# Gate products made early on four row groups and kept in DRAM, GLA and attention regrouped into fewer TensorE visits, x split in halves

## The chip, the cores and the metric

One core of one Trainium2 chip runs the whole program. The metric is the device time of one execution in microseconds (us). TensorE (PE) does the matrix products, VectorE (DVE) and ScalarE (ACT) read its results out of PSUM and do the arithmetic, GpSimd (POOL) helps with sums, and SyncE (SP) issues nearly all DMA transfers, in one queue, in order.

## The reference, cut to what matters

One layer of a decoder over 2048 prompt tokens and 64 sample tokens (8 sequences of 8), 2112 in all, in f32:

```python
z = einsum('btd,dn->btn', x, w_in)              # 1024 -> 6928: q k v g_att gq gk gv g_gla g_lr r_att r_gla
o_att = swa(q, k, v, cache, sink, rel_table)    # 8 heads of 64, 2 KV heads, window 128, blocks of 128
log_a = log_sigmoid(g_lr @ w_gk_up + b_gk) / 16 # the gate product: rank 16 -> 512 = 4 heads x 128
# GLA, 4 heads, state S (128 x 256) carried from chunk to chunk, b = cumsum(log_a) in the chunk:
qt, kt, kend = q * exp(b), k * exp(-b), k * exp(b_last - b)
o = qt @ S + tril(qt @ kt.T) @ v
S = exp(b_last) * S + kend.T @ v
o_gla = rms_norm(o) * gla_norm_w
h = sigmoid(r_att) * ((o_att * silu(g_att)) @ w_pa) + sigmoid(r_gla) * ((o_gla * silu(g_gla)) @ w_pg)
y = layer_norm(alpha * x + h @ w_o)
```

The state of the 8 sample sequences is updated too, and keys, values and states are returned.

## The kernel before, in words

**Dense stream.** The big projections are eight passes, in this order: AT (attention's q, k, v and gate), G0, G1, G2 (GLA's k, q, v and gate for the four heads), PA (w_pa), RA, RG (the merge gates), PG (w_pg); a last stage multiplies by w_o. Each pass uses a seven-product Strassen-like scheme, so it has 21 units (7 products `i` x 3 token ranges `s` of 2 x 352 tokens), and a unit has 5 (AT) or 4 output blocks `p`. One block is one **group**: 12 matmuls of 128x128 weights on 352 columns (L1164 to L1166; 6 in PA), because every f32 operand is split into a rounded high part and a rest (`split`, L146: a cast on ACT, then a subtraction on DVE), and hi*hi, hi*lo, lo*hi are summed. The units' token side is read from DRAM (`raw_x`, L197), and split into `xh` and `xl` of 128x1408 (`prep_x`, L221) one unit ahead; some split pairs are kept in DRAM (`sp_d`) and only reloaded. Results go to DVE and ACT (`combine`, L251), which read them from four PSUM banks named `pd`.

**Side work.** After every group (every second one in PA) `tick()` advances a counter and traces what was put on that count with `at(t, fn)`. So a **visit** of TensorE to side work stands between two groups, and "n ticks later" means n groups later. All side work shares four other PSUM banks, `pa`. TensorE's order is exactly the traced one (`manual_schedule`); the order on the other engines and in SP's queue is chosen by the framework's scheduler when the program is built.

- *Setup and low-rank gate input*, in pass AT: `xcombo` (L553) makes g_lr and stores it to `gl_d` (DRAM, 32 rows: 16, twice).
- *Attention*, in G0 (`ta` = two ticks before G0): 16 blocks, one each SB = 7 ticks. At the block's tick o: `att_scores(.., 0)`, at o+1 `att_scores(.., 2)` (L614: 4 products each on 64-row halves of the array, two banks each; softmax follows behind the second on DVE and ACT), at o+6 and o+7 `att_trans` for each KV head (L651: 8 transposes, two banks each), at o+9 `att_out` (L666, one bank).
- *GLA*, from G1's second half to PG: four heads one after another (`chain`, L1031), 16 tiles of 128 tokens each, one tile each `st` = 4.36 ticks, in 9 chunks per head (`GCH`: 7 of 256 tokens, one of 128, one of 128 + 64). Per chunk: `gla_load` (L858: g_lr rows and k, q), `gla_z` (L878: the gate product for 32 rows x up to 256 columns on TensorE, then log-sigmoid, cumulative sum and exponentials on ACT and DVE), `gla_kq`. Per tile: **v** = `gla_v` (L921: three transposes, one bank, copied out by ACT at L929), **a** = `gla_a` (L934: one product, one bank, masked out by DVE at L939), **b** = `gla_b` (L952: three products of 256 columns, two banks: the output `op`, normalized by ACT and POOL, and the new state `sp`, taken up by DVE at L967), **c** = `gla_c` (L971: two transposes, one bank, multiplied out by DVE at L977).

f32 products of the side work run as two passes on TensorE, and transposes as one.

```python
    def tick():                                          # L132
        while side.get(now[0]):
            side[now[0]].pop(0)()
        now[0] += 1
    ...
            b = t0 + st * (c0 // P)                      # L1039, in chain
            at(b - 14, lambda B=B: gla_load(B))
            at(b - 10, lambda B=B: gla_z(B))
    ...
                at(o, lambda B=B, i=i: gla_v(B, i))
                at(o + st / 4, lambda B=B, i=i: gla_a(B, i))
                at(o + 3 * st / 4, lambda B=B, i=i: gla_b(B, i))
                at(o + 15 * st / 8, lambda B=B, i=i: gla_c(B, i, P, i * P))
```

Of the kernel before, what the change touches and what calls it, by code (L numbers as in the profile page):

```python
# [16 lines left out]
ALU = mybir.AluOpType  # L17
# [40 lines left out]
def kernel(ctx, tc, io):  # L58
# [96 lines left out]
    class Pass:  # L155
# [314 lines left out]
    as_per = const.tile([NS, NS], F32, name="asper")  # L470
    wg = const.tile([P, KT, 32], F32, name="wg")
    for t, n in ((wg, "w_glr"), (cmask, "c_causal"), (smask, "c_scausal"), (bsel, "c_bsel"),
# [332 lines left out]
    for c in range(NP // AT):  # L805
# [41 lines left out]
    def unit(dt=F32, name="u"):  # L847
        return mt("u", GU, 10, dt, name)

    def pair(name):  # L850
        return mt("pr2", 2 * GU, 5, F32, name).rearrange("p (m t) -> p m t", m=2)

    def gla_w(h):
        w = mt("wgk", HK, 2)[:32]
        nc.sync.dma_start(w, io["w_gk"][:, h * HK:(h + 1) * HK])
        R["wgk"] = w

    def gla_load(B):  # L858
        t0, T_ = B["t0"], B["T"]
        g = B["gin"] = unit(name="gin")[:32]  # L860
        nc.sync.dma_start(g[:, :T_], gl_d[:, t0:t0 + T_])
        need(z_kq[B["h"]], range(2), t0, t0 + T_)
# [15 lines left out]
    def gla_z(B):  # L878

        h, T, Tp, nt, last = B["h"], B["T"], B["Tp"], B["nt"], B["last"]  # L880
        ps = pa()
        mm(ps[:, :T], R["wgk"], B["gin"][:, :T], start=True, stop=True)
# [148 lines left out]
    def chain(h, t0, st):  # L1031

        at(t0 - 14, lambda: gla_w(h))
        for c, (c0, T_) in enumerate(GCH):
            last = c == len(GCH) - 1
            Tp = T_ - (NS if last else 0)
            nt = Tp // P
            B = dict(h=h, t0=c0, T=T_, Tp=Tp, nt=nt, last=last)
            b = t0 + st * (c0 // P)  # L1039
# [3 lines left out]
            at(b - 4, lambda B=B: gla_kq(B))  # L1043
            for i in range(nt):
                o = b + st * i
                at(o, lambda B=B, i=i: gla_v(B, i))
                at(o + st / 4, lambda B=B, i=i: gla_a(B, i))
                at(o + 3 * st / 4, lambda B=B, i=i: gla_b(B, i))
                at(o + 15 * st / 8, lambda B=B, i=i: gla_c(B, i, P, i * P))
            at(b + 3, lambda B=B: gla_load_g(B))  # L1050
            o = b + st * nt
            if last:
                at(o - 5, lambda B=B: samp_state(B))
                at(o - st / 2, lambda B=B: gla_v(B, B["nt"]))
                at(o, lambda B=B: samp_a(B))
                at(o + 1, lambda B=B: nc.sync.dma_start(io["o_sp"][B["h"]], R["S"][sstate[B["h"]]]))
                at(o + 3, lambda B=B: samp_b(B, 0))
                at(o + 5, lambda B=B: samp_b(B, 2))
                at(o + 9, lambda B=B: gla_c(B, "s", NS, B["Tp"]))
                at(o + 9, lambda B=B: gla_store(B))  # L1060
# [343 lines left out]
```

## Time and profile before

| | us |
|---|---|
| runs | 1905.35 median of 3 (1904.52 to 1917.58) |
| profiled execution | 1907.78, its span 1905.9 |
| PE busy | 1797.3 of the span |
| DVE, ACT, POOL busy | 1281.0, 841.6, 416.0 |
| pass AT | 4.7 to 245 |
| G0 (attention) | 245 to 500 |
| G1, G2, PA, RA, RG | 500, 732, 955, 1073, 1307 to 1534 |
| PG, last stage | 1534 to 1700, 1700 to 1906 |

In a row of the timeline stand the start, the duration, the engine, the source line and the tiles. A matmul's end is modelled and overlaps the next one's start, so costs are read from start to start.

### The profile page before, as it was taken

What the parts mean: (1) busy time and instruction counts of PE and PEld (TensorE: products, weight loads), DVE (VectorE), ACT (ScalarE), POOL (GpSimd) and SP (SyncE); (2) the same over time, 40 slices, a digit from 0 to 9 for tenths busy, and PEclk for the clock granted to TensorE, in tenths of its full rate; (3) what the DMA queues carried; (4) which work ended last, traced back from release to release, by engine and by line L of the source; (5) the groups of instructions that cost most, each with busy time, mean ns of one, the idle gap of its engine ahead of it and who ended that gap; (6) DMA issues with size and microseconds to landing.
All of it is one profiled execution on the core that took longest, in us unless ns stands there. A gap on an engine that the chain in (4) does not pass through costs nothing. (4 is left out here: it accounts for less than half of the span.)

```text
span 1905.9 us, 30394 instructions
## 1 busy us (share of the span) xinstructions
PE 1797.3 (94%) x10619; PEld 1634.6 (86%) x10619; DVE 1281.0 (67%) x2489; ACT 841.6 (44%) x1762; POOL 416.0 (22%) x554
## 2 busy tenths in 40 slices
PE   7999998899999989999999989998989999899998
PEld 6889996788788979899988888997889999897886
DVE  5648756778667554557568777886667766866656
ACT  3333343545454245555565655675557442311100
POOL 1242012101101002220123132024340224441111
PEclk9999999999999989999999999999999999999999
DMA  9958988868769788878776976688876878796431
GB/s 304 308 198 259 352 318 293 309 226 295 271 232 325 245 264 282 307 249 288 245 229 192 290 257 217 207 279 268 268 260 210 298 278 300 254 310 216 156 116 56
DMA packets 284537, 487.54 MB, mean 256 GB/s; under 512 B 27949, under 2 KB 212133, under 8 KB 284368
## 3 DMA queue, kind: packets, MB, share of 16 engines
q1 hardware_dynamic: 283456, 484.75, 75.5%
q8 instruction: 84, 1.38, 0.3%
q0 software_dynamic: 832, 0.72, 0.2%
q14 instruction: 69, 0.57, 0.1%
q10 hardware_dynamic: 96, 0.13, 0.0%
HBM read 333.73 MB, written 152.64 MB: 255 GB/s over the span
## 5 line engine op out<-in xcount | busy, mean ns | idle before, releaser
L1164 PE MATMUL pd<-xh,wh 128*128 128x352 f32 x2484 | 849.1, 342 | 23.2 <-ACT xh L147 12.8
L1165 PE MATMUL pd<-xl,wh 128*128 128x352 f32 x2484 | 809.6, 326 | 13.0 <-DVE xl L148 12.7
L1166 PE MATMUL pd<-xh,wl 128*128 128x352 f32 x2484 | 809.0, 326 | 0.0
L1164 PEld LDWEIGHTS pd<-xh,wh 128*128 128x128 f32 x2484 | 475.5, 191 | 73.5 <-issue 35.2
L1165 PEld LDWEIGHTS pd<-xl,wh 128*128 128x128 f32 x2484 | 477.6, 192 | 18.2 <-DVE xl L148 17.0
L1166 PEld LDWEIGHTS pd<-xh,wl 128*128 128x128 f32 x2484 | 475.0, 191 | 0.0
L182 POOL TENSOR_TENSOR ws<-ws 128x256 f32<-128x256 f32 (+1 forms) x256 | 205.7, 827 | 681.1 <-DMA ws<-w_g 261.0
L147 ACT CAST wh<-ws 128x512 fp32r<-128x512 f32 (+1 forms) x231 | 134.5, 591 | 213.9 <-POOL ws L182 118.1
L148 DVE TENSOR_TENSOR xl<-xs,xh 128x1408 fp32r<-128x1408 f32 (+1 forms) x114 | 175.5, 1539 | 65.9 <-ACT xh L147 61.5
L148 DVE TENSOR_TENSOR wl<-ws,wh 128x512 fp32r<-128x512 f32 (+1 forms) x231 | 158.6, 693 | 80.5 <-ACT wh L147 75.2
L147 ACT CAST xh<-xs 128x1408 fp32r<-128x1408 f32 (+1 forms) x114 | 143.3, 1258 | 85.5 <-PE pd L1165 74.3
L947 POOL TENSOR_SCALAR sq<-sq 128x1 f32<-128x1 f32 (+1 forms) x68 | 23.7, 349 | 461.4 <-ACT ring L946 461.3
L1210 PE MATMUL pd<-woh,x 128*128 128x512 f32 x256 | 101.7, 397 | 0.7 <-DVE x L148 0.5
L1211 PE MATMUL pd<-wol,x 128*128 128x512 f32 x256 | 101.2, 395 | 0.6 <-DVE wol L148 0.6
L1209 PE MATMUL pd<-woh,x 128*128 128x512 f32 x256 | 101.3, 396 | 0.4 <-ACT woh L147 0.4
L949 ACT ACTIVATE ring<-pa,sq 128x256 f32<-128x256 f32 (+1 forms) x68 | 32.1, 473 | 118.1 <-POOL sq L948 118.1
L147 ACT CAST x<-xst 128x384 fp32r<-128x384 f32 (+2 forms) x48 | 22.3, 486 | 140.3 <-PE pd L1210 107.4
L639 ACT ACTIVATE s<-s,nm 128x256 f32<-128x256 f32 (+1 forms) x128 | 62.4, 489 | 40.1 <-DVE nm L636 40.1
L284 DVE TENSOR_TENSOR a<-a,pd 128x352 f32<-128x352 f32 x93 | 47.7, 519 | 34.2 <-PE pd L1166 34.1
L259 DVE TENSOR_TENSOR fin<-a,pd 128x352 f32<-128x352 f32 x99 | 50.7, 516 | 27.6 <-PE pd L1166 23.7
L280 DVE TENSOR_TENSOR fin<-a,pd 128x352 f32<-128x352 f32 x93 | 48.2, 518 | 27.2 <-PE pd L1166 19.8
L256 ACT COPY a<-pd 128x352 f32<-128x352 f32 x99 | 43.4, 450 | 51.4 <-PE pd L1166 51.4
(248 smaller groups left out, 2581.3 us busy)
## 6 DMA issues: line engine op xcount, KB each, us to landing
xs<-xc_d SPq DMA_DIRECT2D x45, 704.0 KB
ws<-w_g SPq DMA_DIRECT2D x108, 256.0 KB
xs<-xT SPq DMA_DIRECT2D x27, 704.0 KB
xc<-tt_d SPq DMA_DIRECT2D x48, 352.0 KB
ws<-w_at SPq DMA_DIRECT2D x45, 256.0 KB
ws<-w_ra SPq DMA_DIRECT2D x36, 256.0 KB
ws<-w_rg SPq DMA_DIRECT2D x36, 256.0 KB
ws<-w_pg SPq DMA_DIRECT2D x36, 256.0 KB
```

The source lines that it names most:

```text
L147: pin["a"] = nc.scalar.copy(dst_h, src)
L148: i = eng.tensor_tensor(dst_l, src, dst_h.bitcast(F32), ALU.subtract)
L182: nc.gpsimd.tensor_tensor(o[:, c], x[:, c], y[:, c], op)
L259: add(z, acc[p, s, 12], ps, ALU.add)
L280: add(z, u, ps, ALU.add)
L639: nc.scalar.activation(sl, sl, AF.Exp, bias=nm[:, h:h + 1], accum_out=sm[:, h:h + 1])
L1164: mm(ps, wh[:, ks], xh[:, ts], start=(k == 0), stop=False)
L1165: mm(ps, wh[:, ks], xl[:, ts], start=False, stop=False)
L1166: mm(ps, wl[:, ks], xh[:, ts], start=False, stop=(k == q.kh - 1))
L1209: mm(ps, xh[:, xs], hi, start=(k == 0), stop=False)
L1210: mm(ps, xl[:, xs], hi, start=False, stop=False)
L1211: mm(ps, xh[:, xs], lo, start=False, stop=(k == KT - 1))
```

## The change

1. *Gate products.* `gate` makes the gate product of all four heads in five visits, in pass AT (ticks 57, 61, 65, 69, 73), 512 columns at a time: each head's 32 rows stand on another quarter of the partitions, so the four products go to four row groups of the array and to four `pa` banks. ACT and DVE copy them out and SP stores them to `zg_d` (DRAM, 128 x 2112 per head). `gla_z` now reads a loaded slice of `zg_d` and has no product; it stands 8 ticks ahead of its chunk instead of 10, and its load still 14.
2. *Attention.* Both `att_scores` of a block stand in one visit (four banks), both `att_trans` in one visit (four banks); `att_out` as before.
3. *GLA.* v and a of a tile stand at the same tick, and c of the tile three before as well: visit **A** (three banks). b stands 5/4 tile steps behind its v, one or two ticks after the next tile's A: visit **B** (two banks). The sample work at a head's end moves by 2 ticks, stores and the last combinations by 1 to 5.
4. *x split.* `prep_x` makes `xh` and `xl` in two halves of the columns, each a cast and a subtraction.
5. Buffers: one more `u` and one more `pr2` slot, `wg` moved to a pool.

```diff
+    zg_d = [dram.tile([P, NT], F32, name=f"zg{h}_d") for h in range(GH)]
...
-            split(*hl, x)
+            m = self.kh * T // 2
+            for c in (slice(0, m), slice(m, 2 * m)):
+                split(hl[0][:, c], hl[1][:, c], x[:, c])
...
+    def gate_load(c):
+        t0, n = c * 512, min(512, NT - c * 512)
+        if c == 0:
+            GW["w"] = w4(name="wgk")[:, :HK]
+            for h in range(GH):
+                nc.sync.dma_start(GW["w"][32 * h:32 * h + 32], io["w_gk"][:, h * HK:(h + 1) * HK])
+        GW[c] = w4(name="gin")[:, :n]
+        for h in range(GH):
+            nc.sync.dma_start(GW[c][32 * h:32 * h + 32], gl_d[:, t0:t0 + n])
+
+    def gate(c):
+        t0, n = c * 512, min(512, NT - c * 512)
+        ps = [pa() for _ in range(GH)]
+        for h in range(GH):
+            r = slice(32 * h, 32 * h + 32)
+            mm(ps[h][:, :n], GW["w"][r], GW[c][r], start=True, stop=True, tile_position=(32 * h, 0))
+        for h in range(0, GH, 2):
+            z = w4(name="zg").rearrange("p (a t) -> p a t", a=2)
+            nc.scalar.copy(z[:, 0, :n], ps[h][:, :n])
+            nc.vector.tensor_copy(z[:, 1, :n], ps[h + 1][:, :n])
+            for j in range(2):
+                nc.sync.dma_start(zg_d[h + j][:, t0:t0 + n], z[:, j, :n])
+
+    for c in range(-(-NT // 512)):
+        at(t0 + 22 + 4 * c, lambda c=c: gate_load(c))
+        at(t0 + 27 + 4 * c, lambda c=c: gate(c))
...
-            at(o + 1, lambda c=c, bi=bi: att_scores(c, bi, 2))
+            at(o, lambda c=c, bi=bi: att_scores(c, bi, 2))
             at(o + 6, lambda c=c, bi=bi: att_trans(c, bi, 0))
-            at(o + 7, lambda c=c, bi=bi: att_trans(c, bi, 1))
+            at(o + 6, lambda c=c, bi=bi: att_trans(c, bi, 1))
...
-        nc.sync.dma_start(g[:, :T_], gl_d[:, t0:t0 + T_])
+        nc.sync.dma_start(g[:, :T_], zg_d[B["h"]][:, t0:t0 + T_])
...
-        ps = pa()
-        mm(ps[:, :T], R["wgk"], B["gin"][:, :T], start=True, stop=True)
+        z = B["gin"]
...
+            tt = lambda v: t0 + st * v + 0.01
+            b = tt(u)
             at(b - 14, lambda B=B: gla_load(B))
-            at(b - 10, lambda B=B: gla_z(B))
+            at(b - 8, lambda B=B: gla_z(B))
...
+                at(tt(u + i), lambda B=B, i=i: gla_v(B, i))
+                at(tt(u + i), lambda B=B, i=i: gla_a(B, i))
+                at(tt(u + i + 5 / 4), lambda B=B, i=i: gla_b(B, i))
+                at(tt(u + i + 3), lambda B=B, i=i: gla_c(B, i, P, i * P))
```

On PE, before, the side work of about two GLA tiles of head 1 stood like this (`aper` is the masked product, `ring` the state or the normalized output, `ak` and `gv` the copied transposes, `wgk` the gate weights; the groups of dense matmuls between the visits are left out):

```order
5108 L975 MATMUL pa<-ident,ring 128x128 x2
5109 L959 MATMUL pa<-ring,gb 128x256
5110 L961 MATMUL pa<-gv 128x256
5111 L962 MATMUL pa<-gv,aper_206 128x256
5112 L882 MATMUL pa<-gin,wgk 128x192
...
5125 L927 MATMUL pa<-ident,zvv 128x128 x2
5126 L928 MATMUL pa<-ident,ek 128x128
...
5139 L937 MATMUL pa<-dm,em 128x128
...
5164 L959 MATMUL pa<-ring,gb 128x256
5165 L961 MATMUL pa<-ak 128x256
5166 L962 MATMUL pa<-ak,aper_207 128x256
```

In the changed program the same engine has this there (L1003 is c, L955 and L956 v, L965 a, L987 to L990 b):

```order
5203 L1003 MATMUL pa<-ident,ring 128x128 x2
5204 L955 MATMUL pa<-ident,zvv 128x128 x2
5205 L956 MATMUL pa<-ident,ek 128x128
5206 L965 MATMUL pa<-dm,em 128x128
...
5219 L987 MATMUL pa<-ring,gb 128x256
5220 L989 MATMUL pa<-ak 128x256
5221 L990 MATMUL pa<-ak,aper_209 128x256
```

The gate product is gone from this place; visit A fills three of the four `pa` banks, and visit B stands one group (12 matmuls) behind it and takes two. Before, b stood two to three groups behind the visit before it, and a visit with v often one group behind b.

In pass AT, SP's queue now holds the gate's loads and stores between the stores of the pass's results:

```order
124 L596 DMA gin<-gl_d 32x512 x4
125 L219 DMA xs<-xc_d 128x1408
126 L300 DMA z_kv<-fin 128x352
127 L609 DMA zg_d<-zg 128x512 x4
128 L300 DMA z_q_85<-fin 128x352
129 L300 DMA z_q_86<-fin 128x352
```

Before, at the same results, the queue already held weights of pass G0, which it now issues later:

```order
118 L297 DMA z_q_86<-fin 128x352
119 L172 DMA ws<-w_g 128x512 x3
120 L308 DMA z_ga_87<-fin 128x352
121 L172 DMA ws<-w_g 128x512 x2
122 L218 DMA xs<-xc_d 128x1408
```

So 44 transfers are added to this stretch (4 of weights, 20 loads of up to 64 KB, 20 stores of up to 256 KB), and prefetched weights move behind them.

More of the change, by code (lines that the diff above doesn't have):

```diff
@@ L470 @@
     as_per = const.tile([NS, NS], F32, name="asper")
-    wg = const.tile([P, KT, 32], F32, name="wg")
+    wg = mt("wg", KT * 32, 1).rearrange("p (k c) -> p k c", c=32)
     for t, n in ((wg, "w_glr"), (cmask, "c_causal"), (smask, "c_scausal"), (bsel, "c_bsel"),
@@ L580 @@
     at(t0 + 20, setup2)
+    GW = {}
+    def gate_load(c):
[19 more added lines that the diff above has]
+                nc.sync.dma_start(zg_d[h + j][:, t0:t0 + n], z[:, j, :n])
+                wrote(zg_d[h + j], 0, slice(t0, t0 + n))
+    for c in range(-(-NT // 512)):
+        at(t0 + 22 + 4 * c, lambda c=c: gate_load(c))
+        at(t0 + 27 + 4 * c, lambda c=c: gate(c))
     AS = {}
@@ L847, in unit @@
     def unit(dt=F32, name="u"):
-        return mt("u", GU, 10, dt, name)
+        return mt("u", GU, 11, dt, name)
     def pair(name):
[L851 to L856, printed above, removed]
+        return mt("pr2", 2 * GU, 6, F32, name).rearrange("p (m t) -> p m t", m=2)
     def gla_load(B):
         t0, T_ = B["t0"], B["T"]
-        g = B["gin"] = unit(name="gin")[:32]
-        nc.sync.dma_start(g[:, :T_], gl_d[:, t0:t0 + T_])
+        need(zg_d[B["h"]], [0], t0, t0 + T_)
+        g = B["gin"] = unit(name="gin")
+        nc.sync.dma_start(g[:, :T_], zg_d[B["h"]][:, t0:t0 + T_])
         need(z_kq[B["h"]], range(2), t0, t0 + T_)
@@ L880, in gla_z @@
         h, T, Tp, nt, last = B["h"], B["T"], B["Tp"], B["nt"], B["last"]
-        ps = pa()
-        mm(ps[:, :T], R["wgk"], B["gin"][:, :T], start=True, stop=True)
+        z = B["gin"]
         a, b = unit(name="ga"), unit(name="gb")
-        nc.scalar.activation(a[:, :T], ps[:, :T], AF.Abs, bias=bgk[:, h:h + 1])
-        nc.vector.tensor_scalar(b[:, :T], ps[:, :T], bgk[:, h:h + 1], 0.0, op0=ALU.add, op1=ALU.min)
+        nc.scalar.activation(a[:, :T], z[:, :T], AF.Abs, bias=bgk[:, h:h + 1])
+        nc.vector.tensor_scalar(b[:, :T], z[:, :T], bgk[:, h:h + 1], 0.0, op0=ALU.add, op1=ALU.min)
         nc.scalar.activation(a[:, :T], a[:, :T], AF.Exp, scale=-1.0)
@@ L1031, in chain @@
     def chain(h, t0, st):
-        at(t0 - 14, lambda: gla_w(h))
         for c, (c0, T_) in enumerate(GCH):
@@ L1038, in chain @@
             B = dict(h=h, t0=c0, T=T_, Tp=Tp, nt=nt, last=last)
-            b = t0 + st * (c0 // P)
+            u = c0 // P
+            tt = lambda v: t0 + st * v + 0.01
+            b = tt(u)
             at(b - 14, lambda B=B: gla_load(B))
-            at(b - 10, lambda B=B: gla_z(B))
             at(b - 10, lambda B=B: gla_load_v(B))
-            at(b - 4, lambda B=B: gla_kq(B))
+            at(b - 8, lambda B=B: gla_z(B))
+            at(b - 3, lambda B=B: gla_kq(B))
             for i in range(nt):
[L1045 to L1051, printed above, removed]
+                at(tt(u + i), lambda B=B, i=i: gla_v(B, i))
+                at(tt(u + i), lambda B=B, i=i: gla_a(B, i))
+                at(tt(u + i + 5 / 4), lambda B=B, i=i: gla_b(B, i))
+                at(tt(u + i + 3), lambda B=B, i=i: gla_c(B, i, P, i * P))
+            at(tt(u + 1) + 3, lambda B=B: gla_load_g(B))
+            o = tt(u + nt)
             if last:
                 at(o - 5, lambda B=B: samp_state(B))
[L1054 to L1060, printed above, removed]
+                at(o, lambda B=B: gla_v(B, B["nt"]))
+                at(o + 2, lambda B=B: samp_a(B))
+                at(o + 3, lambda B=B: nc.sync.dma_start(io["o_sp"][B["h"]], R["S"][sstate[B["h"]]]))
+                at(o + 5, lambda B=B: samp_b(B, 0))
+                at(o + 7, lambda B=B: samp_b(B, 2))
+                at(o + 11, lambda B=B: gla_c(B, "s", NS, B["Tp"]))
+                at(o + 12, lambda B=B: gla_store(B))
             else:
-                at(b + st * (nt + 7 / 8) + 1, lambda B=B: gla_store(B))
+                at(tt(u + nt + 2) + 1, lambda B=B: gla_store(B))
     tg = max(tick_of(P_G1) + 2, t_att + 3)
@@ L1074 @@
     for j in range(6):
-        at(tg + 17 + 3 * HS + 16 + 5 * j, lambda: combo("u", nc.gpsimd))
+        at(tg + 17 + 3 * HS + 18 + 5 * j, lambda: combo("u", nc.gpsimd))
     for s in range(MS):
         for j in range(2):
-            t = tg + 17 + 3 * HS + ST * (2 * (s + 1) * T / P) + 10 + 2 * j
-            at(t if s < MS - 1 else t_end + 6 + 2 * j, lambda: combo("u", nc.vector))
+            t = tg + 17 + 3 * HS + ST * (-(-2 * (s + 1) * T // GT) * GT // P + 2) + 3 + 2 * j
+            at(t if s < MS - 1 else t_end + 9 + j, lambda: combo("u", nc.vector))
     at(tick_of(P_PG) - 1, lambda: mpool("cm"))
```

## The prediction

> **What bounds the kernel now.** I read the page first, for who is busy:
>
> ```profile
> span 1905.9 us, 30394 instructions
> PE 1797.3 (94%) x10619; PEld 1634.6 (86%) x10619; DVE 1281.0 (67%) x2489; ACT 841.6 (44%) x1762; POOL 416.0 (22%) x554
> ```
>
> TensorE is busy 94% of the span, DVE 67%, ACT 44%. So the time is TensorE's list of work, in its fixed order, plus what it waits for. The list of TensorE's waits comes second (us in total, times, longest):
>
> ```profile
> PE pd L1164 <- ACT xh L147: 12.8, 7, 4.7
> PE pd L1165 <- DVE xl L148: 12.7, 10, 3.9
> PE pa L962 <- DVE aper L939: 12.0, 11, 2.1
> PE pa L882 <- DMA gin<-gl_d: 11.5, 3, 5.3
> PE pa L659 <- DVE s L649: 7.2, 3, 4.2
> PE pa L1164 <- ACT xh L147: 5.5, 2, 4.0
> PE pa L975 <- ACT ring L949: 4.6, 2, 2.7
> PE pa L1165 <- DVE xl L148: 3.7, 3, 1.3
> ...
> PE pa L961 <- ACT gv L929: 2.6, 1, 2.6
> PE pa L961 <- ACT ak L929: 2.4, 3, 1.4
> ...
> PE pa L927 <- DVE ring L967: 1.9, 2, 1.6
> ```
>
> These rows hold 76.9 us. All the parts of the change meet one of them: the x split (34.7 us, four rows with xh or xl), the gate's load (11.5), attention (7.2) and GLA's small products (23.5, the rows with aper, ring, gv and ak).
>
> A long wait costs more than itself. The stretch behind the 3.9 us wait for xl, and the end of pass AT, read by window:
>
> ```profile
> 304.40:309.20 4.80, 4.80 (x17) 4.80 (x18) 1.88 (x7) 3.39 (x13) 0.98 (x2) 0.50 0.56 205
> 200.00:245.00 45.00, 45.00 (x283) 45.00 (x282) 33.47 (x59) 14.20 (x21) 0.00 (x0) 1.00 0.95 344
> ```
>
> In the first row the granted clock is 0.50 and 17 matmuls take 4.8 us. At 0.16 us each (next fence) they take 2.7, so this wait brought 2.1 us more. In the second the clock is 1.00, TensorE never idles, and the DMA engines are busy 0.95.
>
> **The gate products, step by step.** What a visit costs is read from start to start. A gate visit of before, in the timeline:
>
> ```profile
> 866.80 0.32 PE L1165 MATMUL pd<-xl,wh 128*128 128x352 f32 x1
> 866.96 0.32 PE L1166 MATMUL pd<-xh,wl 128*128 128x352 f32 x1
> 867.21 0.69 PE L882 MATMUL pa<-gin,wgk 32*128 32x256 f32 x2
> 867.83 0.43 PE L1164 MATMUL pd<-xh,wh 128*128 128x352 f32 x1
> 868.10 0.32 PE L1165 MATMUL pd<-xl,wh 128*128 128x352 f32 x1
> ```
>
> Dense matmuls start 0.16 us apart. From 866.96 to 868.10 are 1.14 us, of which two dense steps are 0.32, so the visit costs 0.82 us for two passes of 256 columns. A visit of attention's scores, which uses 64-row halves of the array:
>
> ```profile
> 391.14 0.32 PE L1166 MATMUL pd<-xh,wl 128*128 128x352 f32 x1
> 391.39 1.13 PE L625 MATMUL pa<-kk,zq 64*128 64x256 f32 x8
> 392.45 0.43 PE L1164 MATMUL pd<-xh,wh 128*128 128x352 f32 x1
> 392.72 0.32 PE L1165 MATMUL pd<-xl,wh 128*128 128x352 f32 x1
> ```
>
> 1.58 less 0.32 is 1.26 us for eight passes. If the two halves run side by side, this is four steps and a fixed part, where the gate visit is two steps and a fixed part: a step is (1.26 - 0.82)/2 = 0.22 us and the fixed part 0.38. If they ran one after another, a 256-column step would be 0.07 us, less than half of a dense 352-column one, which I exclude. So entering and leaving a divided array costs about 0.38 us a visit. Visits on the whole array show no such part:
>
> ```profile
> 919.07 0.32 PE L1166 MATMUL pd<-xh,wl 128*128 128x352 f32 x1
> 919.23 0.38 PE L927 MATMUL pa<-ident,zvv 128*128 128x128 f32 x2
> 919.45 0.27 PE L928 MATMUL pa<-ident,ek 128*128 128x128 f32 x1
> 919.48 0.41 PE L1164 MATMUL pd<-xh,wh 128*128 128x352 f32 x1
> 919.72 0.32 PE L1165 MATMUL pd<-xl,wh 128*128 128x352 f32 x1
> ```
>
> 0.65 less 0.32 is 0.33 us for three passes of 128 columns, 0.11 each, half of the 0.22 for 256.
>
> By the code there are 36 gate visits: 28 of 256 columns at 0.82, 4 of 192 at 0.71, 4 of 128 at 0.60: 28.2 us go. Five come, four of 512 columns (2 x 0.44 + 0.38 = 1.26 us) and one of 64 (0.49), if four row groups run side by side as two halves do: 5.5 us. Net **-22.7 us**. Bounds: the four one after another are 3.9 us a visit, 16.6 in all, net -11.6; nothing makes it better than -22.7.
>
> The Trainium skill, page "TensorE: Matmul & The Clock Gate", Part 3 (Measured speedup vs the span model), gives 3.07 times for four row groups at 512 columns, not four. By it the five visits would cost some 1.3 us more (an estimate from that page and the step above), and the sum would be -21.4; no trace here shows four row groups.
>
> **The gate's load.** TensorE waited 11.5 us for `gin` in three waits; the longest was 5.3, so the other two hold 6.2 and one of them is over 3. For two such waits I add two tails like the one above, 4 us. In the changed kernel ACT and DVE wait for the load, not TensorE. Load to use grows from 4 ticks to 6, and behind a late load stand ACT's casts and DVE's sums, on which the dense groups wait only when four `pd` banks are full. Bounds: -15.5 (all goes) to 0 (the same lateness reaches TensorE through those banks). I take **-11**, nearer to the end where it goes, since the slack grew by half.
>
> **Attention.** One visit of scores less per block: 16 x 0.38 = **-6.1 us**. Both transposes in one visit change nothing by themselves (whole array). The next block's scores still stand one group behind the transposes and take their banks, as they did before, so I change nothing on that wait. The softmax behind the scores has 6 ticks before both transposes, where the first had 5 and the second 6. The 7.2 us wait for `s` has bounds -7.2 to +7.2; I take 0.
>
> **GLA.** Fewer visits save nothing here, since they cost nothing by their number. What moves is slack. a to b grows from 2.2 ticks to 5.5, v to b from 3.3 to 5.5, b to c from 4.9 to 7.6. So the waits for aper (12.0), ring of L949 (4.6), gv and ak (5.0) should go: -21.6, with tails up to -26. In their place: visit A fills three of four banks, and visit B, one group later, needs two, so in nearly each of 64 tiles a bank must be emptied by DVE (c's multiplication) or ACT (v's copy) within some 2.5 us. Where before a v visit stood one group behind b, the same happened with L967, and it is the 1.9 us row: two waits. Bounds for the new waits: 0 to 64 x 1.1 us (12.0/11, the mean of the aper waits) = 70. I take 10, nearer to the L967 row, which has this form. -26 + 10 is -16; I take **-13 us**, since some of the old waits will fall on another product. Bounds -26 to +48 (70 less the 21.6).
>
> **x halves.** What a unit waits for, by form:
>
> ```profile
> L147 ACT CAST xh<-xs 128x1408 fp32r<-128x1408 f32 x93 | 126.9, 1366 | 78.7 <-PE pd L1165 67.5 <-issue 4.0 <-PE pd L1166 3.3
> L147 ACT CAST xh<-xs 128x704 fp32r<-128x704 f32 x21 | 16.3, 778 | 6.8 <-PE pd L1165 6.8
> L148 DVE TENSOR_TENSOR xl<-xs,xh 128x1408 fp32r<-128x1408 f32 x93 | 156.1, 1679 | 60.4 <-ACT xh L147 56.2 <-PE pd L1165 1.2 <-PE pd L1166 1.0
> L148 DVE TENSOR_TENSOR xl<-xs,xh 128x704 fp32r<-128x704 f32 x21 | 19.4, 923 | 5.5 <-ACT xh L147 5.2
> ```
>
> The first matmul needs xh, the second xl. Whole, they are ready 1.37 and 3.05 us after the cast begins; in halves 0.78 and 1.70, and the six matmuls on the first half (0.96 us) cover the second half. So a unit that waits gains up to 1.35 us. The four rows hold 22 waits, mostly in pairs, and the 4.7 us one is the kernel's start, which isn't touched: some 11 units, -15 us at most. It costs 2 x 0.778 - 1.366 = 0.19 us on ACT and 0.17 on DVE for each of 93 splits, 18 and 16 us over the kernel; TensorE's work hides them, and without that cover they would be 16 us on DVE's path. Bounds -15 to +16; I take **-7**.
>
> **New traffic in pass AT.** The gate's loads and stores are 5.4 MB (2112 columns x 512 rows x 4 bytes stored, a quarter of that loaded), and prefetched weights move behind them, into the stretch that stands at 0.95 and 344 GB/s. 5.4 MB at that rate are 16 us. Bounds 0 (prefetched far ahead of use) to +16; I take **+4**. SP's 44 issues stand before stores of results that nobody waits for until attention. The new copies (8 of 512 columns on each of ACT and DVE) hide behind dense groups.
>
> **Sum.** -22.7 - 11 - 6.1 - 13 - 7 + 4 = -55.8. Against the profiled execution, 1907.78 us (1.9 outside its span), this is 1852; the median of the runs is 2.4 below that execution, so I say **1850 us**.
>
> **Rivals.**
> - *Waits move and don't go.* The fixed parts alone (22.7 + 6.1) less 4 of traffic: 1880. For it: DVE is at 67% and in order, and what it does late it does late wherever the product stands. Against: 2.2 ticks become 5.5. Chance 0.18.
> - *More goes than I take.* Gate load, x and GLA at their good bounds, no cost in AT: -22.7 - 15.5 - 6.1 - 26 - 15 = 1820. 0.14.
> - *The change doesn't run four row groups at once:* 11.1 us less: 1861. 0.04.
> - *DMA becomes the bound at AT's end*, +16 instead of +4, with one late unit behind it: some 1867. 0.06.
> - *The bank of visit B, slower than before.* Each B finds its bank full for s us. The other parts give 42.8, GLA's old waits 23, so the gain is gone at s = 66/64 = 1.0 us and 1% is lost from 1.3. At s = 1.5 us: 1905 - 66 + 96 = 1935. For it: the aper waits averaged 1.1 us with twice the slack. Against: the one-group case that exists waited 1.9 us in all. Chance 0.04; half as bad, s about 0.9, within 1%: 0.10.
> - *My forecast*, 1835 to 1865: 0.44.
>
> A measurement of this kernel can tell about 1%, 19 us, from no change. Faster than 1886: 0.44 + 0.18 + 0.14 + 0.04 + 0.06 = 0.86; within 1% 0.10; slower 0.04. The range, 1815 to 1886, takes in the forecast and the faster cases and leaves out the last rival's 0.14 above and a few hundredths below.
>
> **What would show it.** In the profile after: the four products of a gate visit start within hundredths of a us, in five visits, and no wait for `gin` on TensorE (a wait on ACT instead is fine); 16 score visits of 16 passes at about 2.1 us; aper gone from the waits; sp's product (`pa` <- ak or gv) waiting for c's or v's copy some 10 us in all; xl waits under half of before; pass AT no longer than 250 us. I am wrong if the waits of sp pass 40 us, if AT grows by over 10, or if the clock's slow stretches come as often as before.

## The result, and the profile after

The changed kernel takes **1884.45 us** (median of 4 runs, 1879.07 to 1890.45) against 1905.35 (1904.52 to 1917.58): ratio **0.9876**, 95% interval 0.983 to 0.993. Measured once more, beside the experiments below, it is 0.9831 (0.981 to 0.985). So the change gains 21 to 34 us, where 55 were forecast. The direction held, the size didn't.

From the page of the changed kernel, its profiled execution (1890.45 us):

```profile
span 1888.7 us, 30578 instructions
PE 1776.7 (94%) x10587; PEld 1632.9 (86%) x10587; DVE 1302.7 (69%) x2613; ACT 857.7 (45%) x1886; POOL 413.1 (22%) x554
```

TensorE's busy time fell by 20.6 us and the span by 17.2, so TensorE waits about as long as before. Its list of waits (us in total, times, longest) says for whom; L989 is sp's product in visit B, L1192 and L1193 are the dense products on xh and xl:

```profile
PE pd L1192 <- ACT xh L148: 19.0, 11, 4.7
PE pa L989 <- DVE sg L1005: 16.1, 10, 4.3
PE pd L1193 <- DVE xl L149: 12.2, 13, 1.9
PE pa L989 <- ACT gv L957: 7.0, 3, 2.6
PE pa L1193 <- DVE xl L149: 6.8, 4, 3.2
...
PE pa L1192 <- ACT xh L148: 3.7, 1, 3.7
...
PE pa L989 <- ACT ak L957: 3.2, 3, 2.2
```

The rows with gin (11.5) and aper (12.0) are gone. In their place stand sg, gv and ak on L989 (26.3), and x is waited for somewhat longer than before (41.7 us, 34.7 before). The slow clock is not rarer either: the mean granted clock is 0.977, and 0.979 before. By pass (start:end, length, then busy time of PE, PEld, DVE, ACT, POOL, granted clock, DMA share, GB/s), AT, G0 and G1 of the kernel before:

```profile
4.70:245.10 240.40, 228.30 (x1377) 211.88 (x1378) 159.72 (x282) 82.06 (x141) 49.84 (x66) 0.98 0.84 287
245.10:499.80 254.70, 234.11 (x1418) 204.11 (x1416) 173.22 (x318) 119.83 (x312) 36.03 (x44) 0.97 0.82 290
499.80:732.10 232.30, 220.03 (x1443) 198.37 (x1441) 147.09 (x311) 98.79 (x256) 18.06 (x26) 0.97 0.79 267
```

and the same three of the changed kernel:

```profile
4.70:255.30 250.60, 235.27 (x1417) 214.24 (x1417) 162.68 (x304) 85.47 (x164) 44.28 (x66) 0.97 0.83 283
255.30:510.60 255.30, 234.46 (x1417) 207.17 (x1417) 180.23 (x337) 122.12 (x329) 35.65 (x44) 0.95 0.86 304
510.60:722.20 211.60, 208.57 (x1427) 191.68 (x1426) 137.70 (x300) 94.28 (x246) 17.39 (x24) 1.00 0.81 283
```

AT is 10.2 us longer, G0 no shorter although attention lost 6 us of visits in it, and G1 20.7 shorter. PG, counted from its first dense matmul to the last stage's, takes 182.4 us and not 174.1 (before, the last stage begins at 1707.8, not at 1700). So three questions: what the gate costs in AT and G0, why GLA's waits were replaced and not removed, and what the halves did.

### The profile page after: what moved, and what is told of

Read it like the earlier page. It is cut to its first block, busy times and chain, and to the rows that moved or that the text cites. A ratio compares the mean times of both kernels' runs of the same rounds, so it can differ in the third digit from the quotient of the medians.

```text
span 1888.7 us, 30578 instructions
## 1 busy us (share of the span) xinstructions
PE 1776.7 (94%) x10587; PEld 1632.9 (86%) x10587; DVE 1302.7 (69%) x2613; ACT 857.7 (45%) x1886; POOL 413.1 (22%) x554
## 4 chain that ended last, share of the span: by engine, by line
PE 59%; DMA 13%; DVE 11%; ACT 6%; POOL 5%; issue 4%; SPq 1%; DVEq 0%; POOLq 0%; ACTq 0%
PE pd L1192 14%; PE pd L1193 13%; PE pd L1194 13%; PE pd L1239 3%; PE pd L1238 3%; PE pd L1237 3%; DMA ws<-w_g 2%; POOL ws L183 2%; DVE xl L149 2%; DMA x<-xT 2%; DMA ws<-w_ra 1%; PE pa L658 1%; PE pa L708 1%; PE pa L692 1%; DVE wl L149 1%
## 5 line engine op out<-in xcount | busy, mean ns | idle before, releaser
L1192 PE MATMUL pd<-xh,wh 128*128 128x352 f32 x2484 | 845.7, 340 | 36.3 <-ACT xh L148 19.0
L1193 PE MATMUL pd<-xl,wh 128*128 128x352 f32 x2484 | 811.3, 327 | 12.5 <-DVE xl L149 12.2
L1192 PEld LDWEIGHTS pd<-xh,wh 128*128 128x128 f32 x2484 | 476.9, 192 | 77.5 <-ACT xh L148 30.7
L1193 PEld LDWEIGHTS pd<-xl,wh 128*128 128x128 f32 x2484 | 478.5, 193 | 20.0 <-DVE xl L149 17.9
L149 DVE TENSOR_TENSOR xl<-xs,xh 128x704 fp32r<-128x704 f32 (+1 forms) x228 | 196.6, 892 | 53.5 <-ACT xh L148 49.9
L148 ACT CAST xh<-xs 128x704 fp32r<-128x704 f32 (+1 forms) x228 | 155.6, 723 | 79.3 <-PE pd L1193 58.5
L975 POOL TENSOR_SCALAR sq<-sq 128x1 f32<-128x1 f32 (+1 forms) x68 | 25.9, 381 | 424.1 <-ACT ring L974 423.9
L283 DVE TENSOR_TENSOR fin<-a,pd 128x352 f32<-128x352 f32 x93 | 47.8, 514 | 22.1 <-PE pd L1194 21.4
```

Of the source, the lines that this page charges most:

```text
L148: pin["a"] = nc.scalar.copy(dst_h, src)
L149: i = eng.tensor_tensor(dst_l, src, dst_h.bitcast(F32), ALU.subtract)
L283: add(z, u, ps, ALU.add)
L1192: mm(ps, wh[:, ks], xh[:, ts], start=(k == 0), stop=False)
L1193: mm(ps, wh[:, ks], xl[:, ts], start=False, stop=False)
```

## The experiments

All ratios are to the kernel before, run beside it on the same chip, and the medians are of this kernel; before was at 1907 to 1911 us in these runs. The changed kernel's own two ratios, 0.9876 and 0.9831, are 0.0045 apart, some 9 us; a smaller difference between kernels that weren't run side by side tells nothing by itself.

| kernel | ratio | 95% interval | median us |
|---|---|---|---|
| gate_only | 0.9971 | 0.9959 to 0.9983 | 1904.55 |
| gate_att | 0.9935 | 0.9917 to 0.9952 | 1896.77 |
| no_halves | 0.9934 | 0.9912 to 0.9956 | 1896.21 |
| halves_only | 1.0002 | 0.9984 to 1.0019 | 1909.92 |
| gate_late | 0.9826 | 0.9791 to 0.9861 | 1874.91 |
| no_zg_store | 0.9799 | 0.9765 to 0.9833 | 1873.30 |
| a_first | 0.9853 | 0.9820 to 0.9887 | 1883.18 |
| b_later | 0.9844 | 0.9810 to 0.9878 | 1879.90 |
| after_again | 0.9831 | 0.9808 to 0.9854 | 1875.84 |
| late_whole | 0.9912 | 0.9891 to 0.9933 | 1892.91 |
| late_b | 0.9801 | 0.9778 to 0.9824 | 1871.31 |
| late_b_diag | 0.9785 | 0.9763 to 0.9807 | 1868.51 |
| old_gla | 0.9923 | 0.9896 to 0.9950 | 1892.54 |
| x_quarters | 0.9882 | 0.9853 to 0.9911 | 1883.72 |
| diag_only | 0.9798 | 0.9764 to 0.9832 | 1867.09 |
| diag_end | 0.9749 | 0.9716 to 0.9783 | 1859.47 |
| gate_nostore | 0.9926 | 0.9898 to 0.9954 | 1894.85 |
| gate_diag | 0.9790 | 0.9759 to 0.9822 | 1869.59 |

### The parts one after another

Four kernels: the gate part alone; with attention's merged visits; with GLA's new places too, x whole; and the halves alone. The buffers of point 5 stay changed in all but the last. In diffs against the changed kernel:

```diff
 no_halves (whole x), gate_att and gate_only:
-            for c in (slice(0, m), slice(m, 2 * m)):
-                split(hl[0][:, c], hl[1][:, c], x[:, c])
+            split(*hl, x)
 gate_att and gate_only: the body of chain() and the ticks of combo("u") as before
-                at(tt(u + i + 5 / 4), lambda B=B, i=i: gla_b(B, i))
+                at(o + 3 * st / 4, lambda B=B, i=i: gla_b(B, i))
 gate_only: attention's ticks o+1 and o+7 as before
```

> The gate part alone on the kernel before: products early and stored, GLA and attention at their old places, x split whole. Fixed cost saved: 36 visits (28.2 us) out, five (5.7 us as measured) in, -22.5; the old wait for gin was 11.5. If the parts simply add and the loss lies in GLA's new order or the halves: -22.5 - 11 + 4, some 1875 us. If the gate's traffic in pass AT and the casts beside it eat the gain (pass AT was 10 us longer in the changed kernel): 1885 to 1890, and AT near 250 us.

> The gate part and attention's merged visits, GLA at its old places, x split whole. By the fixed part of a visit, 16 x 0.38 = 6 us less than with the gate alone. If the waits only move: no less than with the gate alone, and the pass G0 with more wait for xh and xl.

> The changed kernel with x split whole. If the halves bring what was forecast: 7 us more than the changed kernel (1.0 - 0.9876 is then some 0.991 of before). If their shorter wait is used up by more instructions on ACT and DVE and by another order of those queues (five new waits for xh and xl at the end of pass PG, several in G0): the same or up to 10 us less than the changed kernel.

> The kernel before with only x split in halves. Forecast: -7 us (bounds -15 to +16). If each late x gains 1.2 us and nothing else moves: -11 us, with the waits for xh and xl at 22 us in place of 34.7. If the order of ACT's and DVE's queues decides: within 3 us of before, with about as many us of waits for xh and xl as before, at other places.

Measured, in us of 1910: the gate 5.5 (both expected cases, 1875 and 1885 to 1890, are missed), attention 6.9 more (6 expected), GLA's new places 0.2, the halves alone 0. By the intervals, these steps are uncertain by some 2 to 5 us each. The halves on top of all the rest are worth 0.0058 to 0.0103 of before, 11 to 20 us, by the changed kernel's two ratios. So the sum isn't linear: GLA and the halves gain nothing one by one, and together 11 to 20 us, where 20 were forecast.

The lengths of the passes say where each kernel gains and loses (us, one profiled execution each, from a pass's first dense matmul to the next one's):

| kernel | AT | G0 | G1 | G2 | PA | RA | RG | PG | last stage |
|---|---|---|---|---|---|---|---|---|---|
| before | 240.4 | 254.7 | 232.3 | 223.1 | 117.9 | 233.9 | 226.6 | 174.1 | 198.1 |
| gate_only | 249.7 | 263.9 | 218.2 | 217.3 | 115.9 | 237.7 | 230.8 | 174.8 | 196.1 |
| gate_diag | 253.3 | 262.0 | 214.3 | 214.8 | 106.7 | 227.1 | 217.3 | 173.2 | 197.3 |
| changed | 250.6 | 255.3 | 211.6 | 221.0 | 114.7 | 225.5 | 223.5 | 182.4 | 199.4 |
| diag_only | 249.0 | 251.6 | 210.9 | 214.2 | 104.6 | 221.5 | 231.7 | 174.9 | 199.9 |

With the gate alone, G1, G2 and PA are 22 us shorter, close to what was forecast there: 19 of the 36 visits stood in these passes (some 15 us of the 28.2) and 9.3 of gin's 11.5 us of waits, all in G1, where TensorE's waits fall from 12.3 to 4.0 us.

The gate alone lost this gain at two places. First in AT and G0, by window (its profiled execution is 6 us above its median):

```profile
4.70:254.40 249.70, 235.77 (x1416) 214.93 (x1417) 162.06 (x288) 84.56 (x148) 45.23 (x66) 0.98 0.83 284
254.40:518.30 263.90, 240.99 (x1419) 208.76 (x1417) 175.81 (x323) 121.71 (x315) 37.18 (x46) 0.95 0.83 294
```

AT is 9.3 us longer and G0 9.2, though in G0 TensorE has the same work. Second, RA and RG are 8.0 us longer, though 17 gate visits (some 13 us) and 2.2 us of gin's waits had gone from them. The largest waits there:

```profile
PE pa L988 <- DVE aper L965: 11.9, 8, 3.1
PE pa L963 <- DVE ring L993: 7.3, 2, 4.1
PE pa L987 <- ACT ak L955: 6.3, 4, 2.4
PE pa L953 <- ACT ring L975: 3.8, 1, 3.8
```

These four rows hold 29.3 us (L988 and L987 are b's products, L963 a's, L953 v's); all rows in these passes 41, where before they were 26.

What did ACT wait for in these two passes? First the kernel before, then the gate alone; L949 and L975 are the norm's scaling, `sq` its factor from POOL, and L910 the first step of `gla_z` on the loaded gate product:

```profile
ACT ring L949 <- POOL sq L948: 78.6, 34, 7.7
```

```profile
ACT ring L975 <- POOL sq L974: 68.4, 35, 7.1
ACT ga L910 <- DMA gin<-zg_d: 29.4, 13, 4.6
```

The second hold is new: gin no longer stops TensorE, it stops ACT, for 29.4 us in these passes and 63.6 in all, and DVE for 16.0. The load is also four times as large, 128 KB a chunk where g_lr was 32. How this reaches TensorE shows at the longest of the waits above, on ACT, DVE and TensorE:

```profile
1168.61 0.51 ACT L910 ACTIVATE ga<-gin,bgk 128x256 f32<-128x256 f32 x1 [4.60 <-DMA gin<-zg_d]
1171.84 0.69 DVE L149 TENSOR_TENSOR wl<-ws,wh 128x512 fp32r<-128x512 f32 x1 [4.77 <-ACT wh L148]
1172.98 0.80 PE L963 MATMUL pa<-dm,em 128*128 128x128 f32 x2 [4.11 <-DVE ring L993]
```

The weight cast stands behind L910 on ACT, DVE waits for the cast, the new state (`ring`, L993) stands behind that on DVE, and a's bank behind the state.

### The gate's place and its stores

```diff
 gate_late: ticks 198, 205, .. 226 (pass G1), tiles gwk, gi, zg from attention's pool
-        at(t0 + 27 + 4 * c, lambda c=c: gate(c))
+        at((ta + 14 + SB * (11 + c) + 4), lambda c=c: gate(c))
 no_zg_store (on the changed kernel), gate_nostore (on gate_only):
-                nc.sync.dma_start(zg_d[h + j][:, t0:t0 + n], z[:, j, :n])
-        nc.sync.dma_start(g[:, :T_], zg_d[B["h"]][:, t0:t0 + T_])
+        nc.sync.dma_start(g[:, :T_], z_kq[B["h"]][:, 0, t0:t0 + T_])
```

> The changed kernel with the five gate visits moved from pass AT (ticks 57 to 73) into pass G1 (ticks 198 to 226, between attention's visits), their tiles in attention's pool and not in w4. With the gate alone, AT was 9 us and G0 9 us longer than before. If it is the gate's traffic and tiles at the end of AT that make x late there and in G0: AT about 241, G0 about 246, G1 some 6 to 8 longer for the visits, in all 10 to 15 us less than the changed kernel (about 0.980 of before). If the loss is not bound to that place: the same as the changed kernel, with the waits in G1.

> The changed kernel without the gate's stores in pass AT (4.3 MB left out; GLA loads as many bytes of other data, so its output is not the reference's). If the bytes on the DMA engines are what delays x in AT and G0: AT 3 to 5 and G0 about 9 us shorter, in all 10 to 13 less than the changed kernel. If it is ACT's and DVE's casts, the w4 tiles or the order of their queues: within 4 us of the changed kernel.

> The gate alone, without its stores in pass AT (4.3 MB left out; GLA loads as many bytes of other data, so its output is not the reference's). The gate alone was 0.9971, with AT and G0 each 9 us longer than before, of which 5.7 us in AT are the visits. If the stores delay x: G0 back at 251 to 255 and 9 to 12 us less, 0.991 to 0.993. If w4's tiles or the casts do it: 0.996 to 0.998.

G0 of the gate alone without its stores:

```profile
251.80:505.80 254.00, 237.26 (x1418) 206.06 (x1416) 171.42 (x319) 119.70 (x312) 36.06 (x46) 0.96 0.83 294
```

G0 is back at 254.0 (263.9), with 10.9 us of waits for xh and xl (16.8 with the stores, 11.4 before), and AT is 2.3 us shorter. The kernel is 0.0045 of before faster, 8.6 us, near the 9 to 12 expected; by the two intervals it can be 3 to 14. In the changed kernel G0 fell from 255.3 to 242.5 without the stores, and the kernel gains 6 to 15 us. So the 4.3 MB stored at the end of AT cost some 9 us, and most of it **one pass later**, where x and its splits arrive late.

Moving the visits to G1 did free AT (241.8) and G0 (246.8), as expected, but G1 took 10.4 of it back: 222.0 against 211.6. The visits themselves, which cost 5.7 us in AT, are about half of that; TensorE's waits there are 3.4 us in place of 3.0, and the granted clock is 0.98 in place of 1.00. In all 0.9826, against 0.9876 and 0.9831 for the changed kernel: a gain of 1 to 10 us, not told from none. The expected 10 to 15 us weren't reached.

### Visit B's bank, or what stands behind it

```diff
 a_first
-                at(tt(u + i), lambda B=B, i=i: gla_v(B, i))
                 at(tt(u + i), lambda B=B, i=i: gla_a(B, i))
+                at(tt(u + i), lambda B=B, i=i: gla_v(B, i))
-                at(tt(u + i + 3), lambda B=B, i=i: gla_c(B, i, P, i * P))
+                at(tt(u + i + 3), lambda B=B, i=i: at(0, lambda: gla_c(B, i, P, i * P)))
 b_later
-                at(tt(u + i + 5 / 4), lambda B=B, i=i: gla_b(B, i))
+                at(tt(u + i + 3 / 2), lambda B=B, i=i: gla_b(B, i))
```

(In a_first one tile, the last of the second head, is scaled and stored from rows that the next head's first b has overwritten; the instructions are the same.)

> The changed kernel with visit A in the order a, v, c in place of c, v, a, so that sp's product in visit B takes the bank of a, which DVE empties first (128 columns), and not that of c or v. If sp's 26.6 us of waits are the bank's: the 16.1 us behind c's multiplication and most of the 10.2 behind v's copy go, 10 to 20 us less than the changed kernel. If they only stand for DVE being late: they appear as a wait for aper or for op's bank, and the time is within 4 us.

> The changed kernel with visit B two dense groups behind the visit A that fills its bank, not one (u+i+3/2 in place of u+i+5/4). If one group is too short for the bank to be emptied: the waits of sp go, 15 to 25 us less than the changed kernel. If the waits move to the next products (c's wait for ring grows, since c then stands one tick nearer): within 5 us.

Neither is told from the changed kernel (0.9853 and 0.9844, between its 0.9831 and 0.9876). With a first, the 16.1 us behind sg are gone and 15.2 behind aper have come. With B later, sg holds 12.4 and a's wait for the state (`ring`) 9.2. The second theory was right: the waits move. That points to something that holds DVE and ACT, wherever the product stands.

One such hold is seen at this wait, on ACT, POOL, DVE and TensorE of the changed kernel:

```profile
1313.54 0.19 ACT L974 ACTIVATION_READ_ACCUMULATOR ring<-pa 128x1 f32 x1
1318.59 0.48 ACT L977 ACTIVATE ring<-pa,sq 128x256 f32<-128x256 f32 x1 [4.86 <-POOL sq L976]
...
1314.46 2.00 POOL L183 TENSOR_TENSOR ws<-ws 128x256 f32<-128x256 f32 x2 [10.50 <-DVE ga L916]
1316.44 0.39 POOL L975 TENSOR_SCALAR sq<-sq 128x1 f32<-128x1 f32 x1
1317.08 0.96 POOL L422 TENSOR_TENSOR x<-x,x 128x352 f32<-128x352 f32 x1 [0.24 <-DMA x<-ug_d]
1317.99 0.57 POOL L976 TENSOR_TENSOR sq<-sq,mhalf 128x1 f32<-128x1 f32 x1
...
1321.69 0.43 DVE L945 TENSOR_TENSOR ek<-zkq,ek 128x256 f32<-128x256 f32 x1 [0.65 <-ACT ek L930]
1323.18 0.42 DVE L1005 TENSOR_TENSOR sg<-pa,sg 128x256 f32<-128x256 f32 x1
...
1323.65 0.70 PE L989 MATMUL pa<-gv 128*128 128x256 f32 x2 [1.53 <-DVE sg L1005]
```

ACT has the sum of squares at 1313.7 and needs the norm's factor for its next instruction. POOL makes it in two steps (L975, L976), each behind a weight difference or a sum of its own, until 1318.6. For 4.86 us ACT does nothing; the casts, a table load (1.28 us) and the exponentials behind it are late, DVE's product with them (L945) is late, sg behind that, and TensorE waits for sg.

### The norm without the wait for POOL

ACT copies op's rows unscaled; POOL multiplies the identity by the 128 factors; c's products with that matrix scale and transpose in one.

```diff
-        nc.scalar.mul(on[:n], o, sq[:n])
+        nc.scalar.copy(on[:n], o)
+        dg = mt("dg", P, 3)
+        nc.gpsimd.tensor_scalar(dg[:n, :n], ident[:n, :n], sq[:n], None, op0=ALU.mult)
...
-            nc.tensor.transpose(tp[:, m * P:m * P + n], on[:n, m * P:(m + 1) * P], ident[:n, :n])
+            mm(tp[:, m * P:m * P + n], on[:n, m * P:(m + 1) * P], dg[:n, :n], start=True, stop=True)
```

gate_diag has this on gate_only, diag_only on the changed kernel, late_b_diag on late_b (late gate and later B). All have ten `u` tiles, where the kernels they are compared with have eleven; that was not run by itself.

> The gate alone, GLA at its old places, with the norm's factors in c's products (ACT does not wait for POOL). With the gate alone the passes RA and RG had 41 us of waits (26 before). If the hold of ACT behind POOL is what turned gin's saved wait into new ones for ring, aper and ak: RA and RG 25 us or less of waits together, PA some 8 us shorter, in all 10 to 16 us less than the gate alone (0.989 to 0.992). If a wait of 2.2 ticks between a and b decides there: aper's 14 us stay, and the gain is under 5 us.

> The changed kernel with only the norm's factors moved into c's products (ACT copies without waiting for POOL; the u tiles are ten, not eleven). If ACT's waits behind POOL are a cause of GLA's waits in the changed kernel: waits for sg, ring, gv and ak (31 us) under 15, 8 to 15 us less. If the waits go elsewhere, as with the later B: the waits by sum the same, within 4 us.

> Gate in pass G1 and visit B at u+i+3/2. If the two gains are of different passes and add: 11 + 6 us less than the changed kernel, some 0.979 of before, 1870 us. If the later B only moves waits: 0.9826 as with the late gate alone.

> As the run before it, but ACT does not wait for POOL in the norm: it copies op's rows unscaled, POOL multiplies the identity by the 128 factors, and c's two products with that matrix scale and transpose in one. In the changed kernel ACT stood idle 94.6 us before the 68 scalings, behind POOL's weight differences, with casts and copies queued behind it. If GLA's waits on TensorE come from ACT and DVE being held up there, whatever the place of the visits: its waits for sg, ring, gv and ak shrink from some 20 us to under 10, and the time by 8 to 15 us more. If those waits are the bank's and DVE's own load: within 4 us of the run before it, with ACT's idle time gone all the same.

The gate alone gains 0.0181 by it (34 us, its bounds 28 to 41 from the two intervals): 0.9790, **with GLA's visits at their old places**. That is more than the 10 to 16 expected; PA, RA and RG are 33 us shorter. Its waits in RA and RG:

```profile
PE pa L990 <- DVE aper L965: 5.6, 6, 1.9
PE pa L989 <- ACT ak L955: 4.4, 4, 1.6
PE pa L953 <- ACT ring L975: 2.2, 1, 2.2
PE pa L963 <- DVE ring L995: 1.7, 1, 1.7
```

13.9 us where the same four rows had 29.3; all rows 20, where the gate alone had 41. ACT still waits 28.3 us for gin there. So the hold behind POOL costs this kernel some 34 us, but it isn't what the gate brought: it was larger before. With it gone, the hold by gin does less harm. The norm's edit was not run on the kernel before, and no run takes gin's hold away, so what each of the two has of the 23 us lost in RA and RG (8.0 longer, some 15 shorter forecast) stays open. And the groups of the norm's last step on ACT, first the kernel before, then the changed kernel, then gate_diag (busy us, mean ns | idle time before it, and for whom):

```profile
L949 ACT ACTIVATE ring<-pa,sq 128x256 f32<-128x256 f32 (+1 forms) x68 | 32.1, 473 | 118.1 <-POOL sq L948 118.1
```

```profile
L977 ACT ACTIVATE ring<-pa,sq 128x256 f32<-128x256 f32 (+1 forms) x68 | 32.2, 473 | 94.6 <-POOL sq L976 94.6
```

```profile
L975 ACT COPY ring<-pa 128x256 f32<-128x256 f32 (+1 forms) x68 | 24.9, 366 | 1.3
```

The 118 us stood in the profile of before, on an engine that is busy 44% of the time and so looked harmless. The gain comes although c's products now run as two passes: 136 more on TensorE, some 14 us at 0.105 us a pass (an estimate from the 0.11 of the prediction's visit on the whole array).

late_b comes to 0.9801, 0.0030 below the changed kernel beside it, where 0.979 was expected if both gains add and 0.9826 if B's is none: too near to both to tell. In the changed kernel the norm's edit gives 0.9798: 6 to 15 us, as its two measurements are taken, and pass PA is 104.6 us, not 114.7. But visit B still waits 22.1 us for sg, gv and ak, where the changed kernel has 26.3 and 23.6 in its two profiles; under 15 was expected for these rows and ring's. On late_b it gives 0.0016, within the intervals, with 19.4 us of such waits where under 10 were expected. So in the new order the hold behind POOL is not what most of GLA's waits come from. In both kernels G2, PA, RA and PG shrink (by 24 us on late_b), and RG grows, by 8 and 11 us. In RG another hold is longer: DVE waits for the loads of PG's sums (`ug_d`, L422), here in late_b_diag:

```profile
DVE x L422 <- DMA x<-ug_d: 26.3, 5, 12.1
```

In late_b this row is 9.0, in diag_only 13.1 and in the changed kernel 7.1. In diag_only TensorE's longest wait (6.84, for sg) stands behind 9.01 us of it, and one of 4.12 for gv behind 8.66 us in which ACT waits for gin. This is read from the traces; no run takes these holds away.

### The halves and GLA's places

```diff
 late_whole: gate_late with split(*hl, x)
 old_gla: the changed kernel with chain() and the ticks of combo("u") as before
 x_quarters
-            m = self.kh * T // 2
-            for c in (slice(0, m), slice(m, 2 * m)):
+            m = self.kh * T // 4
+            for c in (slice(j * m, j * m + m) for j in range(4)):
```

> The changed kernel once more, beside the others on one chip, so that differences of a few us can be read. As first measured: 0.9876 of before (0.983 to 0.993). If the halves brought nothing here either, as in the kernel before: 0.993, like the kernel with x whole.

> Gate in pass G1, x split whole. With the gate in AT, whole x cost some 11 us more than halves; in the kernel before the halves changed nothing. If halves help where x is late, and x is late because of the gate's traffic at AT's end: here within 4 us of the halves (0.983 to 0.985 of before). If they help everywhere in the new order of visits: 8 to 11 us more than with halves, 0.987 to 0.989.

> The changed kernel with GLA's visits at the places of before (gate, attention and halves stay). With x whole, GLA's new places brought nothing (0.9935 without, 0.9934 with them). If the halves gain only together with the new places (a late x then holds up fewer short copies between two visits): 0.990 to 0.994 of before, 10 to 20 us more than the changed kernel. If the halves gain by themselves once gate and attention are changed: 0.983 to 0.986, as the changed kernel.

> The changed kernel with x split in four pieces. If what counts is how long one instruction holds ACT's and DVE's queue (0.78 and 0.89 us in halves, some 0.48 and 0.50 in quarters): 3 to 8 us less than the changed kernel, GLA's waits for sg, gv and ak below its 24 to 27 us. If what counts is when the first piece is ready for TensorE: 1 to 3 us less, at the waits for xh and xl alone. If the fixed part of an instruction now costs more than the shorter hold gains (two more on each engine for each x): 0 to 8 us more.

Three pairs say where the halves count. At GLA's old places: nothing (1.0002 against before; 0.9923 against gate_att's 0.9935). At the new ones: 0.0086 (16 us, 8 to 11 expected) with the late gate, 0.0058 to 0.0103 without. The waits of visit B with the late gate, x whole:

```profile
PE pa L988 <- DVE sg L1004: 20.8, 11, 4.5
PE pa L988 <- ACT gv L956: 9.5, 3, 3.9
PE pa L988 <- ACT ak L956: 3.9, 3, 1.8
```

and in halves:

```profile
PE pa L990 <- DVE sg L1006: 15.0, 12, 4.4
PE pa L990 <- ACT gv L958: 5.0, 3, 2.3
PE pa L990 <- ACT ak L958: 4.2, 3, 2.2
```

10 us less there, and passes G2, RA and RG 23 us shorter (PA and the last stage give 8 back), while AT and G0, where x itself is waited for, differ by 1.3 us at most. So the halves seem to work by what they let pass: a bank of visit A has to be emptied within one group, and a whole x holds DVE 1.67 us and ACT 1.37 in front of the short copy, a half 0.96 and 0.78. At the old places no bank had to be emptied that soon. That they count only with the new places is shown; this reason is argued. Quarters, which hold the queues for less still, lowered B's waits again (19.8 us with sg, gv and ak) but not the time: 0.9882, the waits for xh rose from 22.7 to 27.3 us.

### The fastest version

diag_end is late_b_diag with the chain's end four ticks earlier:

```diff
-    t_end = tick_of(P_PG) - 12
+    t_end = tick_of(P_PG) - 16
```

> Late gate, later B, norm in c's products, and GLA's chain ended four ticks earlier (so spaced closer by a quarter of a tick a tile). Pass PG took 174 us in every kernel with GLA's old places and 180 to 183 with the new ones. If that comes from the chain's end standing three ticks nearer to PG: PG 174 to 175 and 4 to 6 us less than without the earlier end. If it comes from elsewhere: PG as before, and up to 5 us more in the GLA passes, since the tiles stand closer.

It takes 1859.47 us, 0.9749 (0.9716 to 0.9783): faster than both kernels. Its list of waits begins:

```profile
PE pd L1195 <- ACT xh L148: 19.8, 8, 6.1
PE pa L966 <- DVE ring L998: 17.2, 8, 3.9
```

GLA's one large wait is now a's bank behind the new state on DVE. RG is 222.2 us where late_b_diag had 234.4, PG 174.4 (176.0). But diag_only, with the chain's end where the changed kernel has it, has a PG of 174.9 too. So PG's extra 8 us came at least as much from the held-up chain as from where it ends; the two aren't told apart.

## Why the prediction was right or wrong

- **Gate products, -22.7: the cost of a visit was right.** The eight passes of a visit are one row, and its cost is read as in the prediction:

```profile
161.83 0.32 PE L1194 MATMUL pd<-xh,wl 128*128 128x352 f32 x1
162.08 1.14 PE L603 MATMUL pa<-gin,wgk 32*128 32x512 f32 x8
163.15 0.43 PE L1192 MATMUL pd<-xh,wh 128*128 128x352 f32 x1
163.42 0.32 PE L1193 MATMUL pd<-xl,wh 128*128 128x352 f32 x1
```

  163.42 - 161.83 - 0.32 = 1.27 us (1.26 forecast for four row groups side by side); the five visits cost 5.7 us, 5.5 forecast. By the 3.07 times that the Trainium skill gives in "TensorE: Matmul & The Clock Gate", Part 3, a visit would have been some 1.5 us (the prediction's estimate, 1.3 us over five visits); the trace doesn't show that loss.
- **The gate's load, -11: the step that failed first.** gin left TensorE's list as said, and in G1, G2 and PA visits and waits together gave the 22 us. But the gate alone gained 5.5 us, not 29.7. The step said that ACT and DVE would now wait for the load, and that this reaches TensorE only when four `pd` banks are full. It reached TensorE by GLA's own results on `pa`: ACT stood 29.4 us for gin in RA and RG, casts, state and masks came late behind it, TensorE's waits there grew from 26 to 41 us, and the two passes grew by 8.0 us instead of losing 15. ACT's hold behind POOL (68.4 us there), which the prediction doesn't name, left no slack: without it the same kernel gains 34 us, with gin's hold still there. How the 23 us divide between the two holds is open.
- **New traffic, +4: too small, and at the wrong place.** Without the stores the gate alone is 8.6 us faster (3 to 14), and G0 is where that stands (9.9 by the two profiles). AT's own 9.3 us are for the most part the visits (5.7). The term counts AT alone; the gate's loads in the GLA passes grew too, from 32 to 128 KB a chunk, and have no term. The bound of 16 held; my rule, wrong if AT grows by over 10, was met by 10.2.
- **Attention, -6.1: right.** 6.9 measured. A merged visit costs 2.13 us against two of 1.27.
- **GLA, -13: wrong in its reason.** aper went and sp's new waits came to 26 us, not 10. I sized them from one row of 1.9 us that has the same form, and took a one-group distance as the cause; in a_first and b_later the product's place changes, and as much is waited for elsewhere. With x whole the new places brought 0.2 us.
- **x halves, -7: wrong in its reason too.** The late x were to gain; x is waited for 41.7 us, and the halves alone change nothing. They gain 11 to 20 us where B needs its bank soon. GLA and halves together give 11 to 20 us of the 20 forecast; that this is near is luck, since both reasons were wrong.
- **The rivals.** "Waits move and don't go" (1880, chance 0.18) is nearest to what happened, and its reason is what a_first, b_later and the chains above show: DVE does late what stands late in its queue, wherever the product stands. Its sum fits by luck: the 22.7 us of the gate didn't come as time, and the halves' gain isn't in it. I gave it too little, because I looked at TensorE's waits and not at why ACT and DVE were late. The row with 118 us of ACT's idle time was in the profile. The bank of visit B as a loss did not come; the four row groups ran at once.

In the sum: 5.5 (gate) + 6.9 (attention) + 11 to 20 (GLA with halves) = 23 to 32 us, against 24 and 32 by the two ratios. The last term is itself taken from these two ratios, so the sum closes by its making. Of the signs, AT passed 250 us (250.6) and grew by over 10, the waits for xl rose from 16.4 to 19.0 us instead of halving, and the slow clock came as often as before; the four products of a visit, the score visits and the missing gin were as said.

## What to carry to other kernels

Before a wait on the bounding engine is designed away, follow it two steps back: if the engine waited for is itself idle behind a third one or behind a load, moving the product may only rename the wait, and handing a late load to another engine puts it in front of all that stands in that engine's queue. An idle row of an engine that is half empty can matter when short copies stand behind it; here a two-instruction detour over POOL cost 34 us in one kernel, more than the 28.2 of all gate visits, and 6 to 15 in another. Traffic put into a stretch whose DMA engines were at 0.83 to 0.95 was paid mostly one pass later, so look for its price there too.

## What the runs showed of the hardware

A short wait can be enough for the slow clock. In the changed kernel, two waits of 1.22 and 0.50 us, one right after the other:

```profile
265.23 0.43 PE L1192 MATMUL pd<-xh,wh 128*128 128x352 f32 x1 [1.22 <-ACT xh L148]
266.16 0.49 PE L1193 MATMUL pd<-xl,wh 128*128 128x352 f32 x1 [0.50 <-DVE xl L149]
266.45 0.49 PE L1194 MATMUL pd<-xh,wl 128*128 128x352 f32 x1
```

From 266.16 on matmuls start 0.29 us apart and not 0.16, for some 12 steps, 1.6 us lost on 1.7 us of waiting. At 276.75 the same pair of waits left the steps at 0.16. The Trainium skill, "TensorE: Matmul & The Clock Gate", Part 1 (The HAM clock gate), puts the return to the slow clock behind an idle window of about 3.4 us. Here half of that was enough once and not enough at the next place.
